# Three re-orderings around an MLP: dt weights one step later, block casts behind the last halves, and a weight chunk's sums formed by VectorE in place

## The chip, the cores and the metric

The kernel runs on one core of a Trainium2 chip, with its five engines: TensorE (PE in the profile, PEld its weight loads), VectorE (DVE), ScalarE (ACT), GpSimd (POOL) and SyncE (SP), each of which takes its own instructions in the order written. SP and POOL issue nearly all DMAs here. The metric is the device time of one execution in microseconds (us). Of several runs the median is given.

## The reference

One layer of a decoder trunk on 512 tokens with 16 learned tokens put ahead of them, model width 1024, all in float32. A token mixing with two branches is followed by an MLP:

```python
u = rmsnorm(h, mix_norm_w[i])
proj = u @ w_in[i]
...
dt_raw = proj[..., OFF_DT:OFF_GATE]
...
y_pool = pool_mixer(u_pool, pool_w_group[i], pool_scale[i]) @ w_pool_up[i]
y_ssd = mamba2_branch(z, xbc, dt_raw, ...) @ w_ssd_out[i]
h = h + (gate_pool * y_pool + gate_ssd * y_ssd) @ w_o[i]

v = rmsnorm(h, mlp_norm_w[i])
hid = jax.nn.relu(v @ w_ff1[i])
h = h + (hid * hid) @ w_ff2[i]
...
out = rmsnorm(h, final_norm_w)
return out[:, N_META:]
```

`w_ff1` is 1024 x 4096 and `w_ff2` 4096 x 1024.

## The kernel before

Every float32 operand of a large product is split in two: a rounded high part, cast by ACT (`xh`, `vh`, `whi`, `shi`, `hh`), and the rest, subtracted by DVE (`xl`, `vl`, `wlo`, `slo`, `hl`). A product is then three passes of PE: high by high, low by high, high by low. So each weight block that arrives by DMA gets one cast (L93, or L989 in the MLP's later part) and one subtract (L95, L990) before PE can use it.

**The start.** Activations x come transposed in eight slices `xt[k]` of 128 channels. `x_load(k)` issues the load on SP, `x_split(k)` casts `xh[k]` on ACT (L240) and forms `xl[k]` on DVE (L241), and `bc_step(k)` multiplies the slice on PE (L180 to L183) with the blocks wB and wC. `wdt` holds the 32 columns of `w_in` for dt; it is loaded on SP (L280), multiplied by the norm's weights on DVE (L281), and read by PE in `dt_step` (L249) after slices 3 and 7. `e` (L228, L230) is a small selector matrix, `q` and `sq` are the squares for the norm.

**The end of the mixing and the start of the MLP.** The sums h are turned by PE into PSUM, in parts of which `ptD` is the last. `turned` takes the halves from there: `vh` on ACT (L1094), `vl` on DVE (L1095), `vf` on ACT (L1099). `block()` issues the load of a w_ff1 block and its split (`block_split`, L93 and L95). `ff1_begin(c, f)` makes such a block for half f of hidden pair c, and `ff1_part` multiplies it with vh and vl into `pf` (L127 to L130). The scalings at L1397 multiply the four slices of `ht`, the residual, by `m2` of the norm.

**The rest of the MLP** is done in chunks of 512 hidden units, c = 0 to 7. In chunks 0 to 6, products of 2 by 2 quarters are done in seven products of Strassen's kind (Winograd's form), whose weight operands are the quarters b11, b22, b21 and sums of them:

```python
t1 = b11 + b12;  s3 = b12 + b22;  t2 = t1 + b22;  t4 = t2 + b21
```

For w_ff2 (`f2`), t1 and s3 of a chunk are formed in DRAM by POOL's DMAs, in `weight_sums` (two copies and two transfers that add, L713 to L716 for ("f2", c)), and loaded like the quarters by SP into a pool of four tiles (`quarter`, L1195). `sets` lists which chunk's sums are formed in which order. t2 and t4 are added by DVE in place, onto the tile of t1 (L1439). `prod` (L1359, L1362) multiplies an operand with hh and hl of the chunk into `alpha` or other PSUM tiles; `onto` adds `alpha` to `ht` on DVE (L1066). In the loop over c, `e` is true for the seventh chunk, c == 6. The tiles of one name in the trace are told apart in the order by numbers: `b11_6` is b11 of the seventh chunk.

What sets the order of the instructions on an engine is a scheduler that places them by the program's order and their inputs; `tc.issue_after(x)` holds an instruction until x is placed ahead of it.

Of the kernel before, what the change touches and what calls it, by code (L numbers as in the profile page):

```python
# [11 lines left out]
AF = mybir.ActivationFunctionType  # L12
# [22 lines left out]
V_MIX, V_BG, V_PS, V_CW, V_CB, V_DS, V_SN, V_MN, V_DTB, V_AL = (  # L35
    0, 8, 24, 32, 160, 192, 208, 224, 232, 233)
# [27 lines left out]
def kernel(ctx: ExitStack, tc, xT, x, w, f1, f2, vec, fnw, out):  # L64
    nc = tc.nc
    act, dve, pe, pool = nc.scalar, nc.vector, nc.tensor, nc.gpsimd
# [10 lines left out]
    def block_tiles():  # L77
        b = nblk[0]
        nblk[0] += 1
        return (b, wp.tile([P, 1024], F32, tag="raw", name=f"raw{b}", bufs=3),  # L80
                wp.tile([P, 1024], F32R, tag="whi", name=f"whi{b}"),
                wp.tile([P, 1024], F32R, tag="wlo", name=f"wlo{b}"))

    def block_load(t, c):
        nc.sync.dma_start(t[1][:, c], w[t[0], :, c])

    def block_part(t, c):
        block_load(t, c)
        block_split(t, c)

    def block_split(t, c, behind=None):
        b, raw, hi, lo = t
        act.copy(hi[:, c], raw[:, c])  # L93
        with tc.issue_after(behind.ins) if behind is not None else nullcontext():
            dve.tensor_tensor(lo[:, c], raw[:, c], hi[:, c].bitcast(F32), op=ALU.subtract)  # L95

    def block(behind=None):
        t = block_tiles()
        block_load(t, slice(0, 1024))
        block_split(t, slice(0, 1024), behind)  # L100
        return t[2:]
# [48 lines left out]
    def col(off, i, n=P):  # L150
        return vs[:n, off + i : off + i + 1]
# [61 lines left out]
    q = pre.tile([P, L], F32, name="q")  # L213
# [22 lines left out]
    def x_load(k):  # L236
        nc.sync.dma_start(xt[k], xT[:, k, :])

    def x_split(k):
        act.activation(xh[k], xt[k], AF.Copy, scale=col(V_MIX, k))  # L240
        dve.scalar_tensor_tensor(xl[k], xt[k], col(V_MIX, k), xh[k].bitcast(F32),  # L241
                                 op0=ALU.mult, op1=ALU.subtract)
# [32 lines left out]
    for k in range(2, NK):  # L275
        if k > 2:
            x_load(k)
        x_split(k)
        if k == 2:
            nc.sync.dma_start(wdt.rearrange("p k h -> p (k h)"), w[b, :, : NK * H])  # L280
            dve.tensor_tensor(wdt, wdt, vs[:, V_MIX : V_MIX + NK].unsqueeze(2).to_broadcast([P, NK, H]), op=ALU.mult)  # L281
        if k == 4:
            for t in (wB, wC):
                block_part(t, slice(512, 1024))
        bc_step(k)
        if k % 4 == 3:
            dt_step(k - 3)
        square(k - 2)
# [37 lines left out]
    for i in range(2):  # L326
        pb = psum1(f"pb1_{i}")
        c = slice(3 * i, 3 * i + 3)
# [10 lines left out]
    def dtile(name):  # L339
        return dp.tile([P, W], F32, name=name)  # L340

    v, e, s, s2, pl, dt, acs = (dtile(n) for n in ("dv", "de", "ds", "ds2", "dpl", "ddt", "dacs"))
# [21 lines left out]
    for c in (slice(0, P), slice(P, W)):  # L364
        n = c.stop - c.start
# [275 lines left out]
    def out_part():  # L641
# [40 lines left out]
        for d in range(2, NK):  # L682
# [11 lines left out]
           for n in ("13", "42") for p in "hl" for k in range(4)}  # L694
# [3 lines left out]

    B11, B12, B22, B21 = range(4)
    sets = [("f2", 0), ("f2", 1), ("f1", 0), ("f1", 1), ("f1", 2), ("f2", 2), ("f2", 3), ("f1", 3),  # L700
            ("f2", 4), ("f1", 4), ("f2", 5), ("f1", 5), ("f2", 6)]
    assert len(sets) == f1.shape[0] + f2.shape[0]
    SUMS = {"f1": ("t1", "s3", "t2", "t4"), "f2": ("t1", "s3")}
    wsum = {(*t, n): dram.tile([P, 1040], F32, name="{}{}_{}".format(*t, n))[:, :1024]
            for t in sets for n in SUMS[t[0]]}
# [294 lines left out]
    first = []  # L1000
    for n, d in enumerate(MERGE):
# [10 lines left out]
        wh, wl = block()  # L1012
# [13 lines left out]
    ht = hp_.tile([P, 4, D], F32, name="ht")  # L1026
# [14 lines left out]
    vh = [yp.tile([P, SEQ], F32R, tag="yh", name=f"vh{k}") for k in range(NK)]  # L1041
# [27 lines left out]
    ADD, SUB = ALU.add, ALU.subtract  # L1069
# [14 lines left out]
                o = (kk % 2) * 256 + t * P  # L1084
                pe.transpose(pts[kk // 2][:, o : o + P], ht[:, 2 * T + t, k * P : (k + 1) * P], ident)

    low_end = [None]

    def turned(pts, T, half):
        for kk in range(4):  # L1090
            k = 4 * half + kk
            src = pts[kk // 2][:, (kk % 2) * 256 : (kk % 2) * 256 + 256]
            o = slice(256 * T, 256 * T + 256)
            act.activation(vh[k][:, o], src, AF.Copy, scale=col(V_MN, k))  # L1094
            low_end[0] = dve.scalar_tensor_tensor(vl[k][:, o], src, col(V_MN, k), vh[k][:, o].bitcast(F32),  # L1095
                                                  op0=ALU.mult, op1=ALU.subtract)
        for kk in range(0 if half else 4):
            k = 4 * half + kk
            act.activation(v32[k][:, o], pts[kk // 2][:, (kk % 2) * 256 : (kk % 2) * 256 + 256], AF.Copy,  # L1099
                           scale=col(V_MN, k))  # L1100
# [8 lines left out]
    t1 = wo_split("b11")  # L1109
# [15 lines left out]
    s3 = wo_split("b12")  # L1125
# [27 lines left out]
    turn(ptD, 1, 0, (0,))  # L1153


    def ff1_begin(c, f):
        wh, wl = block()
        return psum1(f"pf{c}_{f}"), wh, wl

    def ff1_part(p, ks, first, last):  # L1160
# [5 lines left out]
    ff1_part(pf[0], range(4, 8), True, False)  # L1166
    turn(ptD, 1, 0, (1,))
    turned(ptD, 1, 0)
    for q in ((1, 1), (0, 1), (1, 0)):
        square_sums(*q)  # L1170
    pf.append(ff1_begin(0, 1))
# [11 lines left out]
    m2 = fa.tile([P, 4], F32, name="m2")  # L1183
# [20 lines left out]
    def ff1_plain(n, parts=(range(NK),)):  # L1204
        r = pair_tile(n)
        for i in range(2):
            if pf:
                ps = pf.pop(0)[0]
            else:
                p = ff1_begin(n, i)  # L1210
                ps = p[0]
                for ks in parts if i else (range(NK),):
                    ff1_part(p, ks, ks[0] == 0, ks[-1] == NK - 1)
                    if ks[-1] < NK - 1 or not i:
                        yield
            ri = flat4(r[:, 2 * i : 2 * i + 2, :])
            act.activation(ri, ps, AF.Relu)
            act.activation(ri, ri, AF.Square)
        left_factors(n, r)
        yield  # L1220
# [173 lines left out]
    dve.tensor_tensor(be, m2, m2, op=ALU.mult)  # L1394
    dve.tensor_scalar(be, be, EPS, None, op0=ALU.mult)
    for t in range(4):
        act.activation(ht[:, t, :], ht[:, t, :], AF.Copy, scale=m2[:, t : t + 1])  # L1397

    sums_of_v(0)

    for c in range(NC - 1):
        z, e = c == 0, c == NC - 2

        n = 2 * c + 3
        a = ff1_plain(n, (range(4), range(4, NK))) if n < PLAIN else ff1_pair(n)
        b = ff1_pair(n + 1) if n + 1 < 16 else iter(())
        slots = [[a] * (1 if n < PLAIN else 2)] * 3 + [[a, b]] + [[b, b]] * 3
        if n < PLAIN:
            slots[3] = [b]

        def between(m=None):

            wt = None
            if not c and len(slots) > 4:
                wt = weights(m)
                behind = splits[-1][1] if len(slots) == 7 else added[0]
                if m == "t2":
                    get("b21")
                if m == "s3":
                    behind = sum_on("t4")  # L1420
                with tc.issue_after(splits[-1][0].ins), tc.issue_after(behind.ins):
                    sums_of_v(8 - len(slots))
            for run in slots.pop(0):
                next(run, None)
            return wt or weights(m)

        raws = {}

        def get(n):
            q = {"b11": B11, "b22": B22, "b21": B21}  # L1430
            if n not in raws:
                raws[n] = quarter(f"{n}_{c}", f2[c, q[n]] if n in q else wsum["f2", c, n])
            return raws[n]

        def sum_on(m):

            if m not in raws:
                o = raws[m] = raws["t1"]
                raws[m, "sum"] = dve.tensor_tensor(o, o, get("b22" if m == "t2" else "b21"), op=ADD)  # L1439
            return raws[m, "sum"]  # L1440

        def weights(m):
            if m in ("t2", "t4"):
                sum_on(m)
            return split(get(m))

        prod(av, c, A11, weights("b11"), True, False)
        onto(0, 0, alpha, ADD)
        prod(q5v, c, S1, between("t1"), z, e)
        if e:  # L1450
            for t in range(2):
                onto(0, 1, q5v[t], ADD, t)
                onto(1, 1, q5v[t], ADD, t)
        prod(av, c, S2, between("t2"), False, False)
        onto(0, 1, alpha, SUB)
        prod(av, c, S3, between("s3"), False, False)
        onto(1, 1, alpha, SUB)
        prod(av, c, A22, between("t4"), False, True)
        onto(1, 0, alpha, ADD)
        prod(p2v, c, A12, between("b21"), z, False)  # L1460
        prod(av, c, S4, between("b22"), True, True)
        onto(0, 1, alpha, ADD)
        for run in slots.pop():
            next(run, None)
        assert next(a, None) is None and next(b, None) is None


    c = NC - 1
# [14 lines left out]
    for t in range(4):  # L1483
        T, st = t // 2, slice((t % 2) * P, (t % 2 + 1) * P)
        n = 0
        for half in range(2):
            parts = [(0, 512)] if half == 0 or t < 3 else [(0, 256), (256, 256)]
            for a, m in parts:
# [3 lines left out]
                i = 0  # L1492
# [4 lines left out]
                for k, seg in ((1, (A11, 3)[T]), (0, (A12, A22)[T])):  # L1497
                    wh, wl = wq[k, half]
                    for p in range(2):
                        x0 = p * 512 + a  # L1500
                        f = i == 0 and not (T == 0 and half == 0) and not a
# [5 lines left out]
                src = ps  # L1507
                if not a:
                    src = ht[:, t, cs]
# [146 lines left out]
```

## Time and profile before

| | before |
|---|---|
| runs | 1003.71, 1002.7, 1003.68 us; median 1003.68 |
| profiled execution | 1003.18 us |
| its span | 1001.4 us |
| mean granted clock of PE | 0.999 |
| instructions in the trace | 15539 |

The span runs from the first instruction to the last in the trace of one execution; the execution's own time is 1.78 us longer. In the rows of a timeline the first number is the start in us from the span's start, the second the duration, then engine, line, operation, and output <- inputs with their shapes. Brackets give how long the engine was idle before and what ended it. "x4" is a group of four instructions in a row. The duration of a matmul is modelled: one of 128x512 is shown with 0.39 us, where successive ones start 0.23 us apart.

### The profile page before, as it was taken

What the parts mean: (1) busy time and instruction counts of PE and PEld (TensorE: products, weight loads), DVE (VectorE), ACT (ScalarE), POOL (GpSimd) and SP (SyncE); (2) the same over time, 40 slices, a digit from 0 to 9 for tenths busy, and PEclk for the clock granted to TensorE, in tenths of its full rate; (3) what the DMA queues carried; (4) which work ended last, traced back from release to release, by engine and by line L of the source; (5) the groups of instructions that cost most, each with busy time, mean ns of one, the idle gap of its engine ahead of it and who ended that gap; (6) DMA issues with size and microseconds to landing.
All of it is one profiled execution on the core that took longest, in us unless ns stands there. A gap on an engine that the chain in (4) does not pass through costs nothing.

```text
span 1001.4 us, 15539 instructions
## 1 busy us (share of the span) xinstructions
PE 993.2 (99%) x6095; PEld 878.3 (88%) x6095; DVE 793.2 (79%) x1147; ACT 602.8 (60%) x840; POOL 88.1 (9%) x148
## 2 busy tenths in 40 slices
PE   9999999999999999999999999999999999999997
PEld 7889898999889998988998888888889999999986
DVE  7988797979736687979789667876988888888885
ACT  8675958595827439483255343368666656656654
POOL 0022101111002011002201001121100000000000
PEclk9999999999999999999999999999999999999999
DMA  7378763678238635417978632879654464454432
GB/s 242 92 281 226 202 185 117 193 188 234 63 104 253 164 99 160 132 38 213 280 203 234 230 105 71 238 194 303 182 189 148 149 189 149 146 187 150 127 105 85
DMA packets 56202, 171.47 MB, mean 171 GB/s; under 512 B 6400, under 2 KB 7744, under 8 KB 55104
## 3 DMA queue, kind: packets, MB, share of 16 engines
q1 hardware_dynamic: 36576, 105.86, 32.5%
q0 software_dynamic: 18832, 63.71, 24.3%
q8 instruction: 48, 0.79, 0.3%
q10 hardware_dynamic: 720, 0.91, 0.3%
q14 instruction: 26, 0.21, 0.1%
HBM read 161.90 MB, written 48.40 MB: 210 GB/s over the span
## 4 chain that ended last, share of the span: by engine, by line
PE 98%; DMA 1%; ACT 0%; DVE 0%; issue 0%; SPq 0%; ACTq 0%
PE px L191 12%; PE px L1291 8%; PE alpha L1359 6%; PE pz L191 6%; PE px L193 6%; PE px L1294 4%; PE alpha L1362 3%; PE pgp L191 3%; PE pz L193 3%; PE pgs L191 3%; PE py L556 2%; PE pso L127 2%; PE po L550 2%; PE wo_alpha L1053 1%; PE pso L128 1%; PE pso L130 1%
## 5 line engine op out<-in xcount | busy, mean ns | idle before, releaser
L93 ACT CAST whi<-raw 128x1024 fp32r<-128x1024 f32 (+2 forms) x98 | 98.5, 1014 | 105.7 <-PE px L193 33.2
L95 DVE TENSOR_TENSOR wlo<-raw,whi 128x1024 fp32r<-128x1024 f32 (+2 forms) x98 | 114.7, 1176 | 50.9 <-ACT whi L93 33.1
L191 PE MATMUL px<-uh,whi 128*128 128x264 f32 (+1 forms) x448 | 113.2, 291 | 0.0
L193 PE MATMUL px<-ul,whi 128*128 128x264 f32 (+1 forms) x448 | 110.5, 285 | 0.0
L191 PEld LDWEIGHTS px<-uh,whi 128*128 128x128 f32 x448 | 84.6, 189 | 1.8 <-issue 1.4
L193 PEld LDWEIGHTS px<-ul,whi 128*128 128x128 f32 x448 | 84.3, 188 | 0.4 <-issue 0.2
L1066 DVE TENSOR_TENSOR ht<-ht,alpha 128x1024 f32<-128x1024 f32 x35 | 42.7, 1219 | 29.1 <-PE alpha L1359 29.1
L989 ACT CAST shi<-rawf 128x1024 fp32r<-128x1024 f32 x42 | 44.2, 1051 | 28.7 <-PE alpha L1362 18.2
L191 PE MATMUL px<-uh,wlo 128*128 128x264 f32 (+1 forms) x448 | 58.5, 283 | 0.0
L191 PEld LDWEIGHTS px<-uh,wlo 128*128 128x128 f32 x448 | 55.9, 188 | 0.0
L1359 PE MATMUL alpha<-shi,hh 128*128 128x512 f32 x140 | 55.2, 394 | 0.0
L1362 PE MATMUL alpha<-shi,hl 128*128 128x512 f32 x140 | 54.7, 391 | 0.0
L990 DVE TENSOR_TENSOR slo<-rawf,shi 128x1024 fp32r<-128x1024 f32 x42 | 51.2, 1218 | 0.6 <-ACT shi L989 0.6
L1294 PE MATMUL px<-vsl,shi 128*128 128x256 f32 x192 | 47.4, 280 | 0.0
L1291 PE MATMUL px<-vsh,shi 128*128 128x256 f32 x192 | 47.4, 281 | 0.0
L193 PE MATMUL pz<-ul,whi 128*128 128x512 f32 x112 | 43.6, 390 | 0.0
L191 PE MATMUL pz<-uh,whi 128*128 128x512 f32 x112 | 43.6, 389 | 0.0
L577 DVE RECIPROCAL rs<-rs 128x128 f32<-128x128 f32 x32 | 27.2, 909 | 13.9 <-ACT rs L575 13.8
L1359 PE MATMUL alpha<-slo,hh 128*128 128x512 f32 x140 | 37.4, 389 | 0.0
L1291 PEld LDWEIGHTS px<-vsh,shi 128*128 128x128 f32 x192 | 36.2, 188 | 0.9
L1294 PEld LDWEIGHTS px<-vsl,shi 128*128 128x128 f32 x192 | 36.1, 188 | 0.9
L1294 PE MATMUL px<-vl,shi 128*128 128x256 f32 x144 | 36.1, 283 | 0.0
(558 smaller groups left out, 2859.1 us busy)
## 6 DMA issues: line engine op xcount, KB each, us to landing
raw<-in_w SPq DMA_DIRECT2D x104, 512.0 KB, 4.4
f_t<-in_f POOLq DMA_DIRECT2D x38, 512.0 KB, 6.7
f_s<-in_f POOLq DMA_DIRECT2D x26, 512.0 KB, 8.6
b<-in_f SPq DMA_DIRECT2D x21, 512.0 KB, 4.6
rawf<-in_f SPq DMA_DIRECT2D x36, 256.0 KB, 3.2
rawf<-f_t SPq DMA_DIRECT2D x36, 256.0 KB, 3.0
abc<-acs_d POOLq DMA_DIRECT2D x8, 1024.0 KB, 7.6
f_t<-f_t POOLq DMA_DIRECT2D x12, 512.0 KB, 4.4
```

Source lines behind the costliest of these rows:

```text
L93: act.copy(hi[:, c], raw[:, c])
L95: dve.tensor_tensor(lo[:, c], raw[:, c], hi[:, c].bitcast(F32), op=ALU.subtract)
L191: pe.matmul(o, wt, rhs[0][k][:, c], start=part == 0 and k == 0, stop=part == 1 and k == NK - 1)
L193: pe.matmul(o, wt, rhs[1][k][:, c], start=False, stop=False)
L577: dve.reciprocal(rs[:, ctok(c)], rs[:, ctok(c)])
L989: splits.append((act.copy(hi, src), dve.tensor_tensor(lo, src, hi.bitcast(F32), op=ALU.subtract)))
L990: dve.tensor_tensor(lo, src, hi.bitcast(F32), op=ALU.subtract)))
L1066: added[0] = dve.tensor_tensor(o, o, src, op=op)
L1291: pe.matmul(ps, m, f[k][0], start=start and not low and k == 0, stop=stop and low == 1 and k == 3, skip_group_check=True)
L1294: pe.matmul(ps, m, f[k][1], start=False, stop=False, skip_group_check=True)
L1359: pe.matmul(ps[t], hh[:, p, seg, st], m, start=bool(first and not low and p == 0), stop=bool(last and low and p == 1), skip_group_check=True)
L1362: pe.matmul(ps[t], hl[:, p, seg, st], m, start=False, stop=False, skip_group_check=True)
```

## The change

Three things are changed.

1. `wdt` is loaded and multiplied at k == 3 and not at k == 2, so behind the load and split of the fourth slice.
2. `turned` also records its last `vh`. The cast and the subtract of the block for pair 1, half 0 are held behind the last `vh` and `vl` of `ptD`, and the four scalings of `ht` behind that `vh`.
3. The seventh chunk's sums of w_ff2 are no longer formed in DRAM. SP loads b11, b12, b22 and b21; DVE adds b12 onto b11 (then t1) and b22 onto b12 (then s3).

```diff
     def block_split(t, c, behind=None):
         b, raw, hi, lo = t
-        act.copy(hi[:, c], raw[:, c])
+        first, behind = behind if isinstance(behind, tuple) else (None, behind)
+        with tc.issue_after(first.ins) if first is not None else nullcontext():
+            act.copy(hi[:, c], raw[:, c])
         with tc.issue_after(behind.ins) if behind is not None else nullcontext():
             dve.tensor_tensor(lo[:, c], raw[:, c], hi[:, c].bitcast(F32), op=ALU.subtract)
...
         x_split(k)
-        if k == 2:
+        if k == 3:
             nc.sync.dma_start(wdt.rearrange("p k h -> p (k h)"), w[b, :, : NK * H])
...
     sets = [("f2", 0), ("f2", 1), ("f1", 0), ("f1", 1), ("f1", 2), ("f2", 2), ("f2", 3), ("f1", 3),
-            ("f2", 4), ("f1", 4), ("f2", 5), ("f1", 5), ("f2", 6)]
+            ("f2", 4), ("f1", 4), ("f2", 5), ("f1", 5)]
...
-            act.activation(vh[k][:, o], src, AF.Copy, scale=col(V_MN, k))
+            high_end[0] = act.activation(vh[k][:, o], src, AF.Copy, scale=col(V_MN, k))
...
-    def ff1_begin(c, f):
-        wh, wl = block()
+    def ff1_begin(c, f, behind=None):
+        wh, wl = block(behind)
...
     turned(ptD, 1, 0)
+    all_halves = (high_end[0], low_end[0])
...
-                p = ff1_begin(n, i)
+                p = ff1_begin(n, i, all_halves if (n, i) == (1, 0) else None)
...
     for t in range(4):
-        act.activation(ht[:, t, :], ht[:, t, :], AF.Copy, scale=m2[:, t : t + 1])
+        with tc.issue_after(all_halves[0].ins):
+            act.activation(ht[:, t, :], ht[:, t, :], AF.Copy, scale=m2[:, t : t + 1])
...
         def get(n):
-            q = {"b11": B11, "b22": B22, "b21": B21}
-            if n not in raws:
+            q = {"b11": B11, "b12": B12, "b22": B22, "b21": B21}
+            if n not in raws and e and n in ("t1", "s3"):
+                o = raws[n] = get("b11" if n == "t1" else "b12")
+                dve.tensor_tensor(o, o, get("b12" if n == "t1" else "b22"), op=ADD)
+            elif n not in raws:
                 raws[n] = quarter(f"{n}_{c}", f2[c, q[n]] if n in q else wsum["f2", c, n])
             return raws[n]
```

PE's instructions keep their order. What moves on the others is shown at three places, each as the rows before and then the rows now; the line numbers of the changed kernel are up to 10 higher.

DVE at the start, from the second `wlo` subtract of the blocks' first half to the first add of squares; xl_147 is the fourth slice's low part and e_166 the selector. Before:

```order
L95 TENSOR_TENSOR wlo_165<-raw_163,whi_164 128x256
L230 TENSOR_TENSOR e_166<-e_166,ident 128x32
L281 TENSOR_TENSOR wdt<-wdt,vs 128x256
L230 TENSOR_TENSOR e_166<-e_166,ident 128x32
L241 SCALAR_TENSOR_TENSOR xl_147<-xt_131,vs,xh_139 128x528
L273 TENSOR_TENSOR q<-q,sq_262 128x528
```

And now:

```order
L97 TENSOR_TENSOR wlo_165<-raw_163,whi_164 128x256
L232 TENSOR_TENSOR e_166<-e_166,ident 128x32
L243 SCALAR_TENSOR_TENSOR xl_147<-xt_131,vs,xh_139 128x528
L232 TENSOR_TENSOR e_166<-e_166,ident 128x32
L283 TENSOR_TENSOR wdt<-wdt,vs 128x256
L275 TENSOR_TENSOR q<-q,sq_262 128x528
```

The low part of the fourth slice passes one add of `e` and the multiply of `wdt`. On SP the load of that slice passes the load of `wdt` in the same way.

ACT at the start of the MLP, from the last `vh` of `ptB`; the `whi` cast is that of block pf1_0 in the first place, then of pf1_1, pf2_0 and pf2_1. Before:

```order
L1094 ACTIVATE vh_6375<-ptB,vs 128x256
L93 CAST whi_6811<-raw_6810 128x1024
L1094 ACTIVATE vh_6375<-ptC_6651,vs 128x256
L93 CAST whi_6844<-raw_6843 128x1024
L1077 ACTIVATE m_3_120,ssum<-ht 128x512
L1094 ACTIVATE vh_6368<-ptD_6681,vs 128x256
L1094 ACTIVATE vh_6370<-ptD_6682,vs 128x256
L1094 ACTIVATE vh_6369<-ptD_6681,vs 128x256
L1094 ACTIVATE vh_6371<-ptD_6682,vs 128x256
L1397 ACTIVATE ht<-ht,m_6787 128x1024
L1099 ACTIVATE vf_6353<-ptD_6681,vs 128x256
```

And now:

```order
L1097 ACTIVATE vh_6369<-ptB,vs 128x256
L1097 ACTIVATE vh_6369<-ptC_6645,vs 128x256
L1080 ACTIVATE m_3_120,ssum<-ht 128x512
L1097 ACTIVATE vh_6362<-ptD_6675,vs 128x256
L1097 ACTIVATE vh_6364<-ptD_6676,vs 128x256
L1097 ACTIVATE vh_6363<-ptD_6675,vs 128x256
L1097 ACTIVATE vh_6365<-ptD_6676,vs 128x256
L95 CAST whi_6805<-raw_6804 128x1024
L1102 ACTIVATE vf_6347<-ptD_6675,vs 128x256
```

Both casts that stood ahead of the `vh` of `ptD` stand behind them, the second one behind the four `vf` too, and the first scaling of `ht` behind the third cast. On DVE the subtracts of these blocks move behind the four `vl` of `ptD` likewise.

DVE in the seventh chunk, from the subtract for its b11. Before:

```order
L990 TENSOR_TENSOR slo95_9314<-b11_6_9311,shi95_9313 128x1024
L1321 TENSOR_TENSOR r14_9129<-r14_9129,px14_0_9130 128x256
L1066 TENSOR_TENSOR ht_6319<-ht_6319,alpha_6790 128x2x512
L990 TENSOR_TENSOR slo96_9350<-rawf78_9346,shi96_9349 128x1024
L1318 TENSOR_TENSOR r14_9129<-r14_9129,px14_1_9131 128x256
L990 TENSOR_TENSOR slo97_9369<-t1_6_9366,shi97_9368 128x1024
L1439 TENSOR_TENSOR t1_6_9366<-t1_6_9366,b22_6_9421 128x1024
```

And now:

```order
L993 TENSOR_TENSOR slo95_9308<-b11_6_9305,shi95_9307 128x1024
L1326 TENSOR_TENSOR r14_9123<-r14_9123,px14_0_9124 128x256
L1440 TENSOR_TENSOR b11_6_9305<-b11_6_9305,b12_6_9360 128x1024
L1440 TENSOR_TENSOR b12_6_9360<-b12_6_9360,b22_6_9416 128x1024
L1069 TENSOR_TENSOR ht_6317<-ht_6317,alpha_6784 128x2x512
L1323 TENSOR_TENSOR r14_9123<-r14_9123,px14_1_9125 128x256
L993 TENSOR_TENSOR slo96_9344<-rawf78_9340,shi96_9343 128x1024
L993 TENSOR_TENSOR slo97_9364<-b11_6_9305,shi97_9363 128x1024
L1449 TENSOR_TENSOR b11_6_9305<-b11_6_9305,b22_6_9416 128x1024
```

Both new adds stand ahead of the add of `alpha` to `ht`, and the second of them reads b22. On SP, b12's load has the place of t1's, b22's keeps its place, and b21's has the place of s3's; the DMAs of ("f2", 6) are gone from POOL.

More of the change, by code (lines that the diff above doesn't have):

```diff
@@ L700 @@
     sets = [("f2", 0), ("f2", 1), ("f1", 0), ("f1", 1), ("f1", 2), ("f2", 2), ("f2", 3), ("f1", 3),
-            ("f2", 4), ("f1", 4), ("f2", 5), ("f1", 5), ("f2", 6)]
-    assert len(sets) == f1.shape[0] + f2.shape[0]
+            ("f2", 4), ("f1", 4), ("f2", 5), ("f1", 5)]
+    assert len(sets) == f1.shape[0] + f2.shape[0] - 1
     SUMS = {"f1": ("t1", "s3", "t2", "t4"), "f2": ("t1", "s3")}
@@ L1085, in turn @@
                 pe.transpose(pts[kk // 2][:, o : o + P], ht[:, 2 * T + t, k * P : (k + 1) * P], ident)
-    low_end = [None]
+    low_end, high_end = [None], [None]
     def turned(pts, T, half):
```

## The prediction

> **What bounds the kernel now.** I read the page first, for the span, the shares of the engines and the chain of work that ended last:
>
> ```profile
> span 1001.4 us, 15539 instructions
> PE 993.2 (99%) x6095; PEld 878.3 (88%) x6095; DVE 793.2 (79%) x1147; ACT 602.8 (60%) x840; POOL 88.1 (9%) x148
> PE 98%; DMA 1%; ACT 0%; DVE 0%; issue 0%; SPq 0%; ACTq 0%
> ```
>
> TensorE (PE) is busy 993.2 of 1001.4 us, and the chain is PE for 98% of the span. DVE, which gets the new work, is busy 79%. So an edit off PE can move the end only where PE stands still before or after it. The second view, the waits of PE, says where it stands still for a named releaser, and these are all its rows (total, times, longest):
>
> ```profile
> PE pdt L233 <- DVE ones_r L138: 1.5, 1, 1.5
> PE px L181 <- DVE xl L241: 0.6, 2, 0.3
> ```
>
> Both lie in the first 12 us; no row names a DMA, and none names the MLP. The third view, the windows by stage, bounds the total (columns: window, length, then busy time of PE, PEld, DVE, ACT, POOL, then granted clock, DMA share, GB/s):
>
> ```profile
> 0.00:30.00 30.00, 27.85 (x225) 24.46 (x226) 22.09 (x45) 22.90 (x39) 0.95 (x7) 1.00 0.73 238
> 640.00:735.00 95.00, 95.00 (x445) 78.93 (x444) 79.69 (x116) 63.91 (x102) 13.58 (x20) 1.00 0.79 216
> 900.00:980.00 80.00, 80.00 (x484) 71.43 (x483) 66.84 (x76) 46.87 (x62) 0.58 (x1) 1.00 0.40 124
> 980.00:1001.40 21.40, 15.42 (x81) 13.11 (x79) 11.63 (x26) 9.71 (x25) 0.00 (x0) 0.95 0.27 100
> ```
>
> PE loses 30.00 - 27.85 = 2.15 us at the start and 21.40 - 15.42 = 5.98 us at the end, after its last matmul, and is busy for every microsecond of the two windows in which the second and third edits lie. What can be won is therefore at most about 2 us, at the start alone. What can be lost is decided by margins, which I take from the timeline around each edit.
>
> **Part 1, the dt weights at the start.** The edit puts the load of x's fourth slice (`xt`) ahead of the load of `wdt`, and on DVE `xl` ahead of one add of `e` and the multiply of `wdt`. The rows of before, the DMA row from the chain of waits and the rest from the timeline:
>
> ```profile
> 4.42 0.33 SPq L280 DMA_DIRECT2D wdt<-in_w  x1
> 4.79 0.91 SPq L237 DMA_DIRECT2D xt<-in_xT  x2
> 4.79 5.08 DMA xt<-in_xT
> 9.77 0.42 DVE L281 TENSOR_TENSOR wdt<-wdt,vs 128x256 f32<-128x256 f32 x1
> 9.90 1.47 ACT L240 ACTIVATE xh<-xt,vs 128x528 fp32r<-128x528 f32 x2 [0.32 <-DMA xt<-in_xT]
> 10.10 0.18 DVE L230 TENSOR_TENSOR e<-e,ident 128x32 f32<-128x32 f32 x1
> 10.68 0.77 DVE L241 SCALAR_TENSOR_TENSOR xl<-xt,vs,xh 128x528 fp32r<-128x528 f32 x1 [0.39 <-ACT xh L240]
> 11.50 0.39 PE L181 MATMUL px<-xl,whi 128*128 128x264 f32 x1 [0.33 <-DVE xl L241]
> 13.02 1.10 PE L249 MATMUL pdt<-xt,wdt 128*32 128x264 f32 x16
> 14.48 0.76 DVE L241 SCALAR_TENSOR_TENSOR xl<-xt,vs,xh 128x528 fp32r<-128x528 f32 x1
> 15.73 0.28 PE L181 MATMUL px<-xl,whi 128*128 128x264 f32 x1
> ```
>
> The slice is on the path: issued at 4.79, landed 5.08 later, cast at 9.90 after ACT had waited 0.32, `xl` at 10.68 after DVE had waited 0.39, and PE had waited 0.33 at 11.50. Issued first it leaves SP 4.79 - 4.42 = 0.37 us sooner. The three waits along the chain allow a shift of the least of 0.32, 0.39 and 0.33, which is 0.32. I take -0.3 us. Its bounds are these. If the transfer is held by the DMA engines (busy share 0.73 in this window) and not by its issue, it lands no sooner and the gain is 0. PE's first matmul can follow by a little more than the wait shown; the two PE waits on `xl` together, 0.6, are the most that I allow. On the other side, the add (0.18) and the multiply (0.42) filled DVE's idle time and now stand behind `xl`, so what follows on DVE is up to 0.60 later. The nearest later user is the `xl` that starts at 14.48, ends at 15.24 and is read at 15.73, a slack of 0.49; so the loss is at most 0.60 - 0.49 = 0.11 us. `wdt` itself has time: by these rows its multiply would stand near 10.36 + 0.77 + 0.18 = 11.3 and end at 11.7, while `dt_step` reads it at 13.02 - 0.3 = 12.7. Range of this term: -0.6 to +0.11.
>
> **Part 2, the order of ACT and DVE at the start of the MLP.** The four `vh` of `ptD` now come ahead of the cast of block pf1_0, and the four scalings of `ht` (L1397) come after them too. Nothing is added. Rows of before, from the timelines of ACT, DVE and PE:
>
> ```profile
> 673.10 1.08 ACT L93 CAST whi<-raw 128x1024 fp32r<-128x1024 f32 x1
> 677.72 0.82 ACT L1094 ACTIVATE vh<-ptD,vs 128x256 fp32r<-128x256 f32 x2
> 679.56 0.86 ACT L1094 ACTIVATE vh<-ptD,vs 128x256 fp32r<-128x256 f32 x2 [1.02 <-DVE vl L1095]
> 680.54 0.48 DVE L1095 SCALAR_TENSOR_TENSOR vl<-ptD,vs,vh 128x256 fp32r<-128x256 f32 x1
> 681.36 1.56 ACT L1099 ACTIVATE vf<-ptD,vs 128x256 f32<-128x256 f32 x4
> 680.32 1.14 ACT L1397 ACTIVATE ht<-ht,m 128x1024 f32<-128x1024 f32 x1
> 685.65 0.39 PE L127 MATMUL pf<-vh,whi 128*128 128x512 f32 x1
> 688.40 1.23 DVE L95 TENSOR_TENSOR wlo<-raw,whi 128x1024 fp32r<-128x1024 f32 x1 [2.25 <-ACT whi L93]
> 689.28 1.98 PE L130 MATMUL pf<-vh,wlo 128*128 128x512 f32 x8
> ```
>
> pf1_0's `whi` was cast at 673.10; behind the last `vh` it starts about 680.42 and ends about 681.5. PE reads it first at 685.65: 4.2 us in hand. Its `wlo`, one subtract of 1.23 after that and after the last `vl` (681.02), is there near 682.8 and is first read at 689.28: 6.5 us in hand. The raw loads behind on SP are released by these casts, and shift by as much, but feed blocks that PE reads later still. The opposite bound: were all of ACT's work around it ahead of the cast, two pairs of `vh` (1.68), four `vf` (1.56) and four scalings (4 x 1.14 = 4.56) from 677.72 on, with the wait of 1.02, the cast would start at 686.54 and end at 687.62, about 2.0 us late. The rows of the order exclude that: only the `vh` stand ahead. PE waits for nothing here, so nothing is won either. I take 0.
>
> **Part 3, the sums of the seventh chunk.** POOL loses four DMAs of 512 KB, SP one load, and DVE gains two adds in place. Rows of before, from the timelines of the engines, with the landing time of such a load from the page:
>
> ```profile
> 927.78 0.33 SPq L1195 DMA_DIRECT2D b<-in_f  x1
> b<-in_f SPq DMA_DIRECT2D x21, 512.0 KB, 4.6
> 938.64 0.42 DVE L1321 TENSOR_TENSOR r<-r,px 128x256 f32<-128x256 f32 x1
> 941.07 1.22 DVE L1066 TENSOR_TENSOR ht<-ht,alpha 128x1024 f32<-128x1024 f32 x1 [2.01 <-PE alpha L1359]
> 942.01 1.05 ACT L989 CAST shi<-t 128x1024 fp32r<-128x1024 f32 x1 [0.80 <-PE px L1294]
> 942.21 1.22 DVE L990 TENSOR_TENSOR slo<-rawf,shi 128x1024 fp32r<-128x1024 f32 x1
> 943.73 0.40 PE L1359 MATMUL alpha<-shi,hh 128*128 128x512 f32 x1
> 944.92 1.23 DVE L1439 TENSOR_TENSOR t<-t,b 128x1024 f32<-128x1024 f32 x1
> 948.86 0.64 PE L1291 MATMUL px<-vh,slo 128*128 128x256 f32 x4
> ```
>
> The same add of 128x1024 stands in the kernel already, at 1.23 us; two are 2.46, or about 2.28 in a row, since on DVE an instruction starts 942.21 - 941.07 = 1.14 after one of this size. In the new order they stand between the add at 938.64 and `ht<-ht,alpha` at 941.07, where DVE waited 2.01 us for PE. The first starts at about 938.97, the second at 940.11, `ht` at 941.25 and not 941.07: 0.18 late, done at 942.47. What is late next is PE's reuse of `alpha` at 943.73, with 1.26 us in hand. Behind that `slo` of the next `rawf` block shifts by the 0.18 and by an add of `r` (0.42 as at 938.64) that now precedes it, against a first use at 948.86, over 5 us after its end. t1's cast on ACT at 942.01 finds its sum done at 940.2. So the cost is 0. Without that hole the two adds would put `ht` at 941.07 + 2.46 = 943.53 and its end at 944.75, so PE would stand 1.0 us: the upper bound, since then everything later has its old place. The second add also needs b22's load, issued at 927.78; at 4.6 us it is there near 932.4, 7.7 us ahead of its use.
>
> The removed DMAs give bandwidth back where PE waits for no transfer: 0. The buffers of the last loads come free with the same subtracts as before, so the last four weight blocks are issued when they were.
>
> **The sum.** -0.3 + 0 + 0 + 0 = -0.3 us on the profiled execution, 1003.18 (1001.4 and 1.78 around it), which is 1002.9. That execution stands 0.5 under the median of the three runs, 1003.68, in which the forecast is 1003.4. The runs spread from 1002.7 to 1003.71. About 0.2%, 2 us, is what a measurement of this kernel can tell from no change.
>
> **Rivals.** *(a) Slower: DVE held by b22.* DVE takes its work in the order written, and behind the second add stand `ht<-ht,alpha` and so PE's next `alpha`. If b22 lands at L after 940.11, `ht` starts 1.14 later and ends at L + 2.36; PE stands still from L = 941.37 on, and by over 2 us from 943.4. That asks for 15.6 us in flight where the row says 4.6, in a stage whose DMA share is 0.40 at 124 GB/s; the removal of traffic speaks against it too. At 945 it would cost 3.6 us: 1007.0. Chance 0.04, which also covers this wait at another tile.
>
> The granted clock is 1.00 in every window up to 980 and 0.95 in the last, where PE idles. [...]
>
> *(b) Faster: the 2 MB that no longer pass through POOL's queue and the memory bring forward loads that PE depends on.* The most that this could give is PE's idle time in the first 30 us, 2.15, and the edit touches none of it: its DMAs ran after 700 us. With the whole start gone it would be 1003.7 - 2.15 = 1001.5. Chance 0.04.
>
> *(c) No change, though a little dearer:* the start costs its +0.11 and the hole on DVE closes, +1.0: 1004.8. This lies within the 0.2%. It gets 0.12, and my own sum 0.80. That the edits do not do what they say is excluded by the order.
>
> **Range and chances.** Low: the lowest run, 1002.7, less the 0.6 of the start, 1002.1. High: the highest run, 1003.71, with +0.11 and +1.0, 1004.8. It leaves out (a) and (b), 0.08. Faster by over 0.2% is (b), 0.04; slower (a), 0.04; within 0.2% the rest, 0.92.
>
> **What would show it.** Right: PE's waits keep one row for `xl` of at most 0.3 us in total, no new row at L1359 or L127; two adds of about 1.23 us of `b` between 938 and 942 with `ht` following at once; window 640 to 980 still full. Wrong: a PE wait on `ht` near 943, a `whi` cast that ends after 685.6, or a row of `b` adds with a DMA behind them as releaser.

## The result: slower by 0.4%, and the profile after

The changed kernel takes 1007.69 us in the median of 6 runs (1005.97 to 1009.16), the kernel before 1003.54 us (1002.7 to 1004.44). The ratio is 1.004, with a 95% interval of 1.003 to 1.0051. The forecast was 1003.4 us and no change. The profiled execution took 1008.17 us. Its page, the first lines:

```profile
span 1006.5 us, 15527 instructions
PE 995.9 (99%) x6095; PEld 879.4 (87%) x6095; DVE 795.7 (79%) x1149; ACT 602.3 (60%) x840; POOL 85.3 (8%) x144
```

DVE has its two adds more, POOL its four DMAs less, and the span is 5.1 us longer. The waits of PE (total, times, longest):

```profile
PE alpha L1364 <- DVE ht L1069: 2.1, 1, 2.1
PE pdt L235 <- DVE ones_r L140: 1.5, 1, 1.5
PE px L183 <- DVE xl L243: 0.6, 2, 0.4
PE pf L132 <- DVE wlo L97: 0.2, 1, 0.2
```

The two rows of before are still there, `xl` included. New are a wait of 2.1 us on DVE's add of `alpha` to `ht`, and a small one on a `wlo`. The windows say in which stage:

```profile
640.00:735.00 95.00, 92.62 (x416) 75.78 (x416) 76.18 (x111) 61.59 (x99) 10.84 (x16) 0.98 0.69 185
900.00:980.00 80.00, 80.00 (x495) 71.97 (x494) 70.26 (x78) 48.65 (x63) 0.58 (x1) 1.00 0.43 132
```

The seventh chunk is full as before. PE lost time in the start of the MLP, and its granted clock there is 0.98. The wait itself, and the clock around it, from the timeline of PE and from narrow windows:

```profile
722.26 0.40 PE L1364 MATMUL alpha<-shi,hh 128*128 128x512 f32 x1
725.02 0.39 PE L129 MATMUL pf<-vh,whi 128*128 128x512 f32 x1
730.03 0.77 PE L1364 MATMUL alpha<-shi,hh 128*128 128x512 f32 x1 [2.14 <-DVE ht L1069]
734.41 0.28 PE L1296 MATMUL px<-vh,shi 128*128 128x256 f32 x1
```

```profile
728.00:730.00 2.00, 0.00 (x0) 0.00 (x0) 1.94 (x3) 2.00 (x4) 0.00 (x0) 0.99 0.80 262
730.00:732.00 2.00, 1.97 (x5) 1.61 (x6) 2.00 (x3) 1.94 (x4) 0.00 (x0) 0.50 0.39 33
732.00:734.00 2.00, 2.00 (x8) 1.59 (x7) 1.63 (x2) 0.77 (x2) 0.00 (x0) 0.66 0.81 301
734.00:736.00 2.00, 2.00 (x17) 1.91 (x16) 1.39 (x2) 0.74 (x1) 0.00 (x0) 1.00 0.96 302
```

After the wait the granted clock is 0.50. A product into `alpha` takes 725.02 - 722.26 = 2.76 us ahead of the wait and 734.41 - 730.03 = 4.38 us behind it: 1.6 us more. The same steps of PE in before, where it has no wait in this stage:

```profile
721.01 0.39 PE L1359 MATMUL alpha<-shi,hh 128*128 128x512 f32 x1
726.45 0.39 PE L1359 MATMUL alpha<-shi,hh 128*128 128x512 f32 x1
729.17 0.28 PE L1291 MATMUL px<-vh,shi 128*128 128x256 f32 x1
```

Start against start, the changed kernel is 722.26 - 721.01 = 1.25 us late at the first of these products, 730.03 - 726.45 = 3.58 us at the second and 734.41 - 729.17 = 5.24 us behind it. So the whole 5.1 us of the span is lost by then: 2.3 us by the wait on `alpha` and 1.7 us by the slow clock behind it. Of the 1.25 us, 0.5 came with the short `wlo` wait. The other 716.28 - 715.57 = 0.7 us stand already at the first product into `q` of this stage, before any of these waits; the profiles of the experiments lie between 715.23 and 717.60 there, with the change's parts in or out, so they are not put down to the change. All this is one execution; in the medians the loss is 1007.69 - 1003.54 = 4.15 us.

Why `ht` is late is read backwards. On DVE, from the timelines, first before, then after:

```profile
688.40 1.23 DVE L95 TENSOR_TENSOR wlo<-raw,whi 128x1024 fp32r<-128x1024 f32 x1 [2.25 <-ACT whi L93]
690.69 0.96 DVE L1339 TENSOR_TENSOR hl<-r,hh 128x768 fp32r<-128x768 f32 x1 [1.06 <-ACT hh L1338]
724.10 1.22 DVE L1066 TENSOR_TENSOR ht<-ht,alpha 128x1024 f32<-128x1024 f32 x1
```

```profile
692.24 1.23 DVE L97 TENSOR_TENSOR wlo<-raw,whi 128x1024 fp32r<-128x1024 f32 x1 [6.28 <-ACT whi L95]
696.05 0.96 DVE L1344 TENSOR_TENSOR hl<-r,hh 128x768 fp32r<-128x768 f32 x1 [2.59 <-ACT hh L1343]
728.67 1.22 DVE L1069 TENSOR_TENSOR ht<-ht,alpha 128x1024 f32<-128x1024 f32 x1
```

DVE stood 6.28 us for the `whi` of the fourth block, pf2_1, and was 5.4 us late with the first `hl`. At the add of `alpha` 33 us later it is still 4.6 us late, because in between it has hardly a hole in which to catch up. The windows of before:

```profile
700.00:710.00 10.00, 10.00 (x46) 8.29 (x45) 9.97 (x15) 7.86 (x11) 1.86 (x3) 1.00 0.69 191
710.00:720.00 10.00, 10.00 (x46) 8.29 (x45) 10.00 (x18) 5.80 (x8) 1.68 (x2) 1.00 0.95 226
```

DVE is busy 9.97 and 10.00 of 10 us there (third figure after the length): as full as PE. One step further back stands ACT, before and then after:

```profile
687.29 1.08 ACT L93 CAST whi<-raw 128x1024 fp32r<-128x1024 f32 x1
689.81 0.85 ACT L1338 CAST hh<-r 128x768 fp32r<-128x768 f32 x1
```

```profile
691.15 1.05 ACT L95 CAST whi<-raw 128x1024 fp32r<-128x1024 f32 x1 [4.79 <-DMA raw<-in_w]
695.19 0.82 ACT L1343 CAST hh<-r 128x768 fp32r<-128x768 f32 x1
```

ACT stood 4.79 us for a load, at the cast of pf2_1, with `hh` and all else of the MLP behind it. And the load, from SP's timelines with the landing times of the `raw` loads of that stage (min, median, max), before and then after:

```profile
676.28 0.33 SPq L85 DMA_DIRECT2D raw<-in_w  x1
DMA to landing us min/median/max: 8.3/8.7/10.4
```

```profile
682.24 0.33 SPq L85 DMA_DIRECT2D raw<-in_w  x1
DMA to landing us min/median/max: 7.8/7.9/8.8
```

There are three raw buffers. The fourth block's load waits until the subtract of the first, pf1_0, has read its own, and the change moved that subtract behind the halves of `ptD`: so the load is issued at 682.24 and not at 676.28. Landing takes 8 to 10 us here, about twice the 4.4 that the page gives for `raw` loads over the whole program. The window from 676 to 692 us of before shows the DMA engines full, at a share of 1.03 and 345 GB/s:

```profile
676.00:692.00 16.00, 16.00 (x75) 13.21 (x74) 9.29 (x19) 14.84 (x25) 2.21 (x3) 1.00 1.03 345
```

The chain of work that ended last, in the trace of the changed kernel, runs through just these steps. Six of its pieces (start, length, what), the ones between them left out:

```profile
682.24 8.83 DMA raw<-in_w
691.15 1.05 ACT whi L95
699.10 0.96 ACT shi L992
700.08 1.02 DVE slo L993
728.75 1.14 DVE ht L1069
730.03 0.77 PE alpha L1364
```

By the timelines the waiting cast is 691.15 - 687.29 = 3.86 us later than in before, and from it to `shi` ACT takes 699.00 - 691.15 = 7.85 us where it took 691.57 - 687.29 = 4.28: three scalings of `ht` stand between the two, and one in before. So the held scalings add to the lateness, standing behind the cast that waits.

### The profile page after: what moved, and what is told of

Same layout as the page of the kernel before. It is cut to its first block, busy times and chain, and to the rows that moved or that the text cites. A ratio compares the mean times of both kernels' runs of the same rounds, so it can differ in the third digit from the quotient of the medians.

```text
span 1006.5 us, 15527 instructions
## 1 busy us (share of the span) xinstructions
PE 995.9 (99%) x6095; PEld 879.4 (87%) x6095; DVE 795.7 (79%) x1149; ACT 602.3 (60%) x840; POOL 85.3 (8%) x144
## 4 chain that ended last, share of the span: by engine, by line
PE 93%; DVE 3%; DMA 2%; ACT 1%; issue 0%; DVEq 0%; ACTq 0%
PE px L193 12%; PE px L1296 8%; PE alpha L1364 6%; PE pz L193 6%; PE px L195 6%; PE px L1299 4%; PE alpha L1367 3%; PE pgp L193 3%; PE pz L195 3%; PE pgs L193 3%; PE py L558 2%; PE pso L129 2%; PE po L552 2%; PE pso L130 1%; PE wo_alpha L1056 1%; PE pgp L195 1%
## 5 line engine op out<-in xcount | busy, mean ns | idle before, releaser
L992 ACT CAST shi<-b 128x1024 fp32r<-128x1024 f32 x25 | 26.2, 1050 | 17.3 <-PE px L1299 14.5
```

What stands on the lines that cost most here:

```text
L992: splits.append((act.copy(hi, src), dve.tensor_tensor(lo, src, hi.bitcast(F32), op=ALU.subtract)))
```

## The experiments

The theory, A: the late load of pf2_1 holds ACT, which works in order, and DVE behind it, and DVE's add reaches PE late. Rivals: B, the new order of casts and scalings does it, whatever the load; C, the adds of the seventh chunk or the missing DMAs; D, PE lacks the late block itself. Each ratio is to the kernel before, run again beside these kernels (medians 1003.53 and 1003.51 us).

**part2_only**: the kernel before with the second part alone (the edits of `block_split`, `turned`, `ff1_begin` and L1397).

> Of the three parts of the change only the second (block pf1_0's cast and subtract and the scalings of ht behind the halves of ptD). Theory A, a late load that holds ACT: this part moves the load of the fourth raw block, pf2_1, about 6 us later, since its buffer is freed by pf1_0's subtract; ACT then waits 4 to 5 us at that block's cast, and PE for DVE near 728 us. Expected 3 to 6 us over the kernel before, 1006.5 to 1009.5, with a PE wait of 1.5 to 3 us on ht <- ht, alpha. Theory C, the new adds in the seventh chunk or the missing DMAs: this kernel takes the time of before, 1003.0 to 1004.4.

Measured: 1007.99 us, ratio 1.0038 (1.0026 to 1.0051). ACT's wait and PE's:

```profile
692.18 1.05 ACT L95 CAST whi<-raw 128x1024 fp32r<-128x1024 f32 x1 [4.49 <-DMA raw<-in_w]
PE alpha L1362 <- DVE ht L1068: 2.2, 1, 2.2
```

The whole loss lies in this part; C falls.

**parts_1_and_3**: the changed kernel without it.

> The change without its second part. Theory A: the time of before within 0.7 us, 1002.8 to 1004.2, and PE busy for all of 640 to 735 us and 900 to 980 us; two adds of b near 940 us with ht <- ht, alpha less than 0.5 us late. Theory C: 1006.5 to 1009.

Measured: 1003.39 us, ratio 1.0001 (0.9992 to 1.0011). DVE in the seventh chunk:

```profile
939.15 2.48 DVE L1433 TENSOR_TENSOR b<-b,b 128x1024 f32<-128x1024 f32 x2
941.54 1.21 DVE L1066 TENSOR_TENSOR ht<-ht,alpha 128x1024 f32<-128x1024 f32 x1
```

The two adds stand within 0.3 us of where the forecast had put them, 2.39 us from the first's start to `ht` where it had 2.28. PE is busy for all of 640 to 735 and 900 to 980 us.

**late_cast**: the load stays late, but ACT does not stand in front of it.

```diff
...
-                p = ff1_begin(n, i, all_halves if (n, i) == (1, 0) else None)
+                p = ff1_begin(n, i, all_halves if (n, i) == (1, 0) else
+                              (hh_at[0], None) if (n, i) == (2, 1) else None)
...
-        act.copy(hh[:, :m, :], r[:, :m, :])
+        hh_at[n] = act.copy(hh[:, :m, :], r[:, :m, :])
```

> The changed kernel, and the cast of the fourth block pf2_1 on ACT is held behind the first cast of hh of the MLP, so that ACT goes on with other work while the load is under way; the load itself is issued as late as in the changed kernel. Theory A (what costs is that ACT stands in line behind a cast that waits): the PE wait near 728 us goes, 1003 to 1004.5. Theory B (what costs is the new order of the casts and scalings on ACT and DVE, the load has nothing to do with it): no better than the changed kernel, 1006.5 to 1009. Theory D (the late block itself is late for PE): a PE wait on its wlo or whi, over 1005.

Measured: 1003.5 us, ratio 0.9998 (0.999 to 1.0007). ACT's timeline:

```profile
690.95 0.86 ACT L1344 CAST hh<-r 128x768 fp32r<-128x768 f32 x1
692.28 1.05 ACT L95 CAST whi<-raw 128x1024 fp32r<-128x1024 f32 x1 [0.47 <-DMA raw<-in_w]
```

The load is issued at 682.85, as late as in the changed kernel, and its block is cast a microsecond later than there; yet the loss is gone. B falls as a cause by itself, since the `vh`, the cast of pf1_0 and the scalings are held as in the changed kernel; the four scalings now run from 685.26 to 691.1, while the load is under way. D falls too: PE waits for no operand of that block.

**sub_only**: on the kernel before, only the subtract that frees the buffer is held. The change's edits of `block_split`, `turned` and `ff1_begin` are in as well, for this one hold.

```diff
...
-                p = ff1_begin(n, i)
+                p = ff1_begin(n, i, all_halves[1] if (n, i) == (1, 0) else None)
```

> The kernel before with one edit: only the subtract of block pf1_0 on DVE is held behind the last vl of ptD; its cast on ACT keeps its place ahead of the vh of ptD and nothing else is held. The subtract frees the raw buffer, so the load of pf2_1 is issued near 682 us and not at 676. Theory A: ACT waits 3 to 5 us for that load at the cast of pf2_1 and the kernel is slower by 2 to 6 us, 1005.5 to 1009.5. Theory B (the order of the casts on ACT): the time of before, 1003 to 1004.4.

Measured: 1005.65 us, ratio 1.0016 (1.0007 to 1.0026).

```profile
690.26 1.05 ACT L95 CAST whi<-raw 128x1024 fp32r<-128x1024 f32 x1 [3.66 <-DMA raw<-in_w]
PE alpha L1362 <- DVE ht L1068: 0.7, 1, 0.7
PE pf L129 <- ACT vh L1096: 0.6, 1, 0.6
```

With pf1_0's and pf1_1's casts in their old places ACT waits 3.66 us and the kernel is slower. The second PE wait is another matter: the scheduler put two scalings ahead of the last `vh`, so half of this loss may be theirs.

**cast_only**: the hold on pf1_0's cast and subtract without the hold on the scalings (the edit at L1397 left out).

> The kernel before with half of the second part: the cast and the subtract of block pf1_0 held behind the halves of ptD, the scalings of ht left free (the scheduler then puts two of them ahead of the vh). Theory A, ACT held by the late load of pf2_1: the hold is enough, 2 to 6 us over before, 1005.5 to 1009.5, with an ACT wait of 3 us or more for raw at the fourth cast. Rival: both holds together are needed, 1003 to 1004.4.

Measured: 1006.17 us, ratio 1.0027 (1.0015 to 1.0038), an ACT wait of 3.81 us for `raw`, and

```profile
PE alpha L1362 <- DVE ht L1068: 1.8, 1, 1.8
```

The hold on the block is enough for a loss. What the held scalings add is not settled: with them free 693.23 - 690.70 = 2.53 us of ACT's time lie from the cast to `hh`, with them held 695.19 - 691.15 = 4.04; the medians are 1.5 us apart, but the two intervals overlap.

**cast_behind_vf**: the hold of the changed kernel moved behind the last `vf`.

```diff
...
-            act.activation(v32[k][:, o], ...
+            full_end[0] = act.activation(v32[k][:, o], ...
...
-                p = ff1_begin(n, i, all_halves if (n, i) == (1, 0) else None)
+                p = ff1_begin(n, i, (full_end[0], low_end[0]) if (n, i) == (1, 0) else None)
```

> The changed kernel with the cast of pf1_0 held behind the last vf and not only the last vh of ptD, so that its subtract, and with it the load of pf2_1, comes 2 to 3 us later still. In the order the cast of pf2_1 then stands later in ACT's queue, directly ahead of the first hh, where the changed kernel has some 4 us of other ACT work between the two. If the time goes with the lateness of the load alone, it is slower than the changed kernel by 2 us or more, 1009 to 1012. If it goes with the time at which ACT gets past the wait to hh and what follows (theory A), hh starts near 694 to 697 as in the changed kernel and the time is 1005.5 to 1009.

Measured: 1003.49 us, ratio 0.9998 (0.9989 to 1.0006). Both expectations missed in the number.

```profile
690.74 1.05 ACT L95 CAST whi<-raw 128x1024 fp32r<-128x1024 f32 x1 [2.34 <-DMA raw<-in_w]
691.69 0.83 ACT L1343 CAST hh<-r 128x768 fp32r<-128x768 f32 x1
PE alpha L1364 <- DVE ht L1069: 0.4, 1, 0.4
```

The load was issued at 683.69, only 1.5 us later than in the changed kernel, and landed in 7.05 us where that one's took 8.8. So the cast starts no later, and `hh` follows it at once where there 4 us of ACT work lay between. That a later load gives a faster kernel speaks against the load's lateness by itself, and for the time at which ACT gets past it to `hh` and what follows.

**part1_only** and **part3_only**: the kernel before with the first part alone (`if k == 3`), and with the third alone.

> The kernel before with the load and multiply of wdt moved from k == 2 to k == 3 and nothing else. The forecast was -0.3 us by an earlier landing of the fourth slice; if the transfer is held by the DMA engines and not by its issue, the wait of PE on xl stays at 0.3 to 0.5 us and the change is 0 to +0.2. Either lies within 0.2%: 1002.9 to 1004.0. What is read is the landing of the fourth slice, the wait of PE on xl and the start of the next windows.

> The kernel before with the sums of the seventh chunk formed by DVE in place and nothing else. Forecast: 0 us, 1003.0 to 1004.2, the two adds in the hole of DVE near 939 to 941.3 us and ht <- ht, alpha 0.2 us late; PE busy for all of 900 to 980 us. If the adds were on the path: +1.0 us with a PE wait at alpha near 944.

Measured: 1003.2 us, ratio 0.9995 (0.9986 to 1.0003), and 1003.62 us, ratio 0.9997 (0.9988 to 1.0005). Neither can be told from no change, and PE is full from 900 to 980 us in both.

**All together.** To compare lateness across traces, I take the start of the first `hh` cast on ACT against the start of the first matmul into `q` on PE, which comes ahead of PE's wait on `alpha`; the difference to that of before (689.81 - 715.57 = -25.76) is how late `hh` is. It stands for ACT's work behind the cast: by the chains of the traces, what hands the lateness to DVE is `shi` in the changed kernel and in part2_only, `hh` in cast_only, and in sub_only the next load, which waits for pf2_1's subtract.

| kernel | hh | q | hh late by, us | PE waits for alpha, us | ratio |
|---|---|---|---|---|---|
| before | 689.81 | 715.57 | 0 | 0 | 1 |
| parts_1_and_3 | 689.88 | 715.76 | -0.1 | 0 | 1.0001 |
| late_cast | 690.95 | 716.87 | -0.2 | 0.3 | 0.9998 |
| cast_behind_vf | 691.69 | 715.23 | 2.2 | 0.4 | 0.9998 |
| sub_only | 693.25 | 716.13 | 2.9 | 0.7 | 1.0016 |
| cast_only | 693.23 | 715.97 | 3.0 | 1.8 | 1.0027 |
| part2_only | 696.23 | 717.60 | 4.4 | 2.2 | 1.0038 |
| changed kernel | 695.19 | 716.28 | 4.7 | 2.1 | 1.004 |

Some 2 us of lateness are absorbed; what goes beyond reaches PE, within 0.8 us either way (late_cast's 0.3 us is at the product after). No kernel beat the one before, and none pointed to one: PE is full there.

## Why the prediction was wrong

**What failed** is one sentence of part 2: the raw loads behind "are released by these casts, and shift by as much, but feed blocks that PE reads later still". The shift was there (676.28 to 682.24, released by the subtract and not the cast). It was weighed only against PE's use of the block, and so its cost was put at nothing. Three numbers of the trace of before were not put beside it. First, the landing: 8.3 to 10.4 us for the loads of this stage, not the page's 4.4 for the program. Second, the place of the cast in ACT's queue: 687.29, ahead of the first `hh`. The sum 682.2 + 8.7 = 690.9 against 687.3 puts the cast 3.6 us late; it was 3.86 late, and ACT, which came to it earlier, waited 4.79. With the page's 4.4 the load would be there at 686.6, and the cast would not be late. Third, the fill of DVE from 700 to 720 us, 9.97 and 10.00 of 10 us, by which the delay stayed. The margins of 4.2 and 6.5 us for pf1_0 itself held: no PE wait shows at its `whi` or `wlo`. The 0.2 us wait on a `wlo` at 721.22 belongs to a later block.

**The bound on a loss** in part 2 (2.0 us, then excluded by the order) bounded the wrong event. The true one was larger and had a second term, the 1.6 us of slow clock, which the sum left out.

**The rivals.** (a) named the right kind of thing, an engine in order behind a wait for a transfer and PE behind its `alpha`, but on DVE in the seventh chunk, with 7.7 us in hand. It happened on ACT, some 250 us earlier. Its 0.04 was given because the margins looked wide at the places that I had looked at.

**Part 1.** The gain of 0.3 us is neither shown nor excluded (part1_only: -0.14% to +0.03%). In the changed kernel the slice was issued at 4.27 and not 4.79, and PE waited longer:

```profile
10.02 0.74 ACT L242 ACTIVATE xh<-xt,vs 128x528 fp32r<-128x528 f32 x1 [1.18 <-DMA xt<-in_xT]
11.61 0.39 PE L183 MATMUL px<-xl,whi 128*128 128x264 f32 x1 [0.41 <-DVE xl L243]
```

That fits the bound that I had named, a transfer held by the engines and not by its issue: from 5 to 10 us of this trace the DMA engines' busy share is 1.00 at 330 GB/s, and the slice landed 5.72 us after its issue, where it had taken 5.08. In part1_only it was issued at 4.49, the same cast began at 9.10, so within 4.61 us, and no such wait is left. So the landing varies between executions by more than the 0.52 us by which the issue moved. The sign that the forecast had named, at most 0.3 us of waits on `xl`, did not come in the changed kernel: they are 0.6 us, as before.

**Part 3** went as worked out: `ht` follows the adds at once and PE does not notice. **The removed DMAs** were worth nothing, as forecast.

## What to carry to other kernels

Where an instruction that frees a buffer is moved, follow the load that waits for that buffer to the first instruction that waits for the load, and ask what stands behind that one in its own engine's queue: the data's last user may be far away and the queue not. Take the landing time from loads of the same stage, with its DMA share beside it. And read the slack of a chain from the engine that is full in the next stage: DVE, busy 9.97 and 10.00 of 10 us in before, did not catch its delay up here but handed it on, 5.4 us at the first `hl` and still 4.6 us at the add of `alpha`.

## What the runs showed of the hardware

The granted clock fell to 0.50 after PE had stood for 2.14 us (changed kernel), and likewise after 2.16 us in part2_only (0.50 from 732 to 734 us); it stayed at 1.00 after 1.8 us in cast_only and 0.7 us in sub_only. In the changed kernel the slow stretch was some 3 us of the 4.38 that the product took: the clock is 0.50 from 730.0 to 733.0 us, 0.63 in the half microsecond after that, and 1.00 from 733.5 on.

These are four profiled executions, and they give no length of wait at which the clock falls. Of the other runs only the mean clock of the whole execution is on record. In the changed kernel the three runs at 0.997 took 1008.17 to 1009.16 us, the three at 0.998 or 0.999 1005.97 to 1007.22. In cast_only, whose profile has no slow stretch, the six runs at 0.997 or less took 1006.25 to 1010.41 us, the other six 1004.88 to 1006.09. So some executions of one kernel seem to pay for the slow clock and others not; no trace of those runs is there to show it.
